# A two-layer hybrid decoder on one core: weight splits, squares, rotary angles and early weight loads put in other places

## The chip, the core and the metric

The kernel runs as one program on one core of a Trainium2 chip. The core has a matrix engine (TensorE, PE in the profile; PEld is its weight load), VectorE (DVE), ScalarE (ACT), GpSimd (POOL) and SyncE (SP), each with its own instruction stream. Every DMA of this kernel is issued from SP. The metric is the device time of one execution in microseconds; of several runs the median counts.

## What is computed

512 tokens of 1024 channels pass through two layers in float32. In each layer:

```python
h = rmsnorm(x, norm_mix_pre)
proj = h @ w_in                      # q, k, v | r, k, v, lora_w, lora_a, lora_g | two gates
q = rope(q, positions); k = rope(k, positions)
y_att = sliding_window_attention(q, k, v, att_sinks) @ w_o_att
y_rw = rwkv7_time_mix(rw, ...) @ w_o_rw
x = x + rmsnorm((sigmoid(gate_a) * y_att + sigmoid(gate_b) * y_rw) @ w_out, norm_mix_post)
h = rmsnorm(x, norm_ffn_pre)
ua, ub = split(causal_dwconv(h @ w_up, conv_w, conv_b))      # 2 x 2816 channels
x = x + rmsnorm((gelu(ua) * ub) @ w_down, norm_ffn_post)
e = p_i @ w_ple                                              # 256 -> 1024: the embeddings
x = x + rmsnorm(sigmoid(x @ w_ple_gate) * e, norm_ple)
```

## The kernel before, in words

**Tiling.** All activations lie channel-first: a tile is 128 channels by 512 tokens, x has eight (KT = 8). A half is 256 tokens (HALVES). Every float32 operand is split into a high and a low part, and a product is three matmuls (`mm3`, lines 245 to 247): high weight by high activation, high by low, low by high. So a projection tile of 1024 channels in is 24 matmuls, of 512 columns or, by halves, of 256.

**A weight's way.** SP issues the DMA of a raw weight into SBUF; ScalarE copies it into the high part (`wh`, or `kwh` where the weight is kept for both halves; line 125 is the helper that issues every ACTIVATE); VectorE subtracts to get the low part (`wl` at line 155, `kwl` at line 128). Raw and split weights go round in buffers by class: "m" has two raw buffers and three of each part, "f" one and two, "x" takes both classes by turns (`whole` and `load_w` take a class, `keep_w` keeps a split weight in a pool given to it, with raws through the slots of "m" and "f"). A DMA whose raw buffer is still being read waits on SP, and everything behind it on SP waits too.

**PSUM.** Tiles are named `pm` (two buffers), `pf` (one), `lead`, `half` and `scores` (three together), `ple` and others (two). A tile gets its buffer when the last reader of the tile before it is done.

**Stages of a layer.** `lead` runs the opening tiles of a projection by halves, so that the first half can begin when half of the tokens are normed: in the mixer the low-rank and key tiles, ahead of the up projection five conv tiles. `seam` ties a norm to such an opening. Behind the mixer's opening stand the low-rank gates (`lora`), then, in layer 0 only, the angles of the rotary embedding (`trig`: sine and cosine of positions, stored through `csd` and read back as `sinT` and `cosT`), then the attention; copies `qs<-q` rotate the halves of q and k. Behind the up projection's opening come eight embedding tiles (`w_ple`, classes "m" and "f" by turns), each copied by ScalarE to `e` and stored to `ed`; then `ffn` with the conv tiles m and 22 + m (FT = 22) by turns. Five conv tiles are done by the opening; the next two, 24 and 3, have their weights loaded at the start of `ffn` (`ahead`). Each conv tile is multiplied on VectorE by the norm's scale (`un<-pf` or `un<-pm`), and three steps make the convolution (`cv`).

**The turn into the gate.** The down projection (`dn`) is a `lin` with seven whole tiles and the last by halves. Between them four of the eight gate weights are kept in advance. `fin` is its result; `post_norm` norms a half of it (`rstd`, then `yo` and `x` on VectorE) and `scaled` splits it into `xh` and `xl`. Then the gate `pg`, a `lin` with deep = 3: tiles 0 to 2 together, then the other five, first for the first half, then for the second, where tiles 3 to 7 use `half` buffers. `ple` is its end: it loads the embedding back (`yo<-ed`), takes the tanh (`tg`) and multiplies. In `turn` the second half's norm stands behind `last_lo`, the last low part made.

**What sets the order.** The text is only a priority: a list scheduler (the Tile framework) sorts instructions of all engines by it. `turn` raises the priority of what is in it, and `tc.issue_after(i)` holds what is in it back until i is issued.

## Time and profile before

| | us |
|---|---|
| median of three runs | 2374.32 (2373.6 to 2386.13) |
| the profiled execution | 2373.8 |
| its span, first to last instruction | 2371.9 |
| TensorE busy | 2228.8 (94%) |
| VectorE busy | 1554.1 (66%) |
| ScalarE busy | 1123.6 (47%) |

TensorE's mean granted clock is 0.971 of full speed. The two levels seen in the rows are 2.4 GHz (1.0) and 1.2 GHz. Busy times overlap between engines; a wait of TensorE counts where nothing else of it can run meanwhile. Rows of the listing in time give start, duration, engine, line, operation, output and inputs, and in brackets the idle time of the engine ahead and what ended it; equal neighbours are one row with xN.

### The profile page before, as it was taken

What the parts mean: (1) busy time and instruction counts of PE and PEld (TensorE: products, weight loads), DVE (VectorE), ACT (ScalarE), POOL (GpSimd) and SP (SyncE); (2) the same over time, 40 slices, a digit from 0 to 9 for tenths busy, and PEclk for the clock granted to TensorE, in tenths of its full rate; (3) what the DMA queues carried; (4) which work ended last, traced back from release to release, by engine and by line L of the source; (5) the groups of instructions that cost most, each with busy time, mean ns of one, the idle gap of its engine ahead of it and who ended that gap; (6) DMA issues with size and microseconds to landing.
All of it is one profiled execution on the core that took longest, in us unless ns stands there. A gap on an engine that the chain in (4) does not pass through costs nothing.

```text
span 2371.9 us, 39518 instructions
## 1 busy us (share of the span) xinstructions
PE 2228.8 (94%) x14340; PEld 1756.5 (74%) x14340; DVE 1554.1 (66%) x3683; ACT 1123.6 (47%) x2450; POOL 27.3 (1%) x86
## 2 busy tenths in 40 slices
PE   7699999999999999999898999998999999999986
PEld 6566776667779788888795667766677888888876
DVE  4765588677566777733777646788666667776355
ACT  4466456445444554532355554555543445444332
POOL 1000000000000000000000000000000000000000
PEclk9899999789999999999899999999999999999998
DMA  3532332335571333333235233333356623333431
GB/s 123 153 91 99 107 94 73 85 97 181 164 249 60 118 101 96 95 116 100 80 124 153 83 104 101 88 94 92 110 158 210 215 70 103 98 98 102 125 98 36
DMA packets 206818, 269.39 MB, mean 114 GB/s; under 512 B 72096, under 2 KB 88992, under 8 KB 206624
## 3 DMA queue, kind: packets, MB, share of 16 engines
q1 hardware_dynamic: 206624, 266.88, 36.5%
q8 instruction: 113, 1.85, 0.3%
q14 instruction: 81, 0.66, 0.1%
HBM read 218.95 MB, written 42.47 MB: 110 GB/s over the span
## 4 chain that ended last, share of the span: by engine, by line
PE 71%; DVE 12%; DMA 8%; ACT 6%; issue 3%; SPq 1%; POOL 0%; DVEq 0%; ACTq 0%; POOLq 0%
PE pm L245 12%; PE pm L247 12%; PE pm L246 12%; PE pf L245 6%; PE pf L247 6%; PE pf L246 6%; DVE wl L155 2%; DMA w<-in_w_dn_dram 1%; PE A L117 1%; ACT wh L125 1%; PE pT L550 1%; PE scores L117 1%; SPq L122 1%; PE xs L773 1%; PE sp L780 1%
## 5 line engine op out<-in xcount | busy, mean ns | idle before, releaser
L125 ACT ACTIVATE wh<-w 128x512 fp32r<-128x512 f32 (+1 forms) x590 | 353.6, 606 | 567.9 <-PE pm L246 172.5
L155 DVE TENSOR_TENSOR wl<-w,wh 128x512 fp32r<-128x512 f32 (+2 forms) x574 | 376.7, 661 | 266.8 <-ACT wh L125 261.7
L247 PE MATMUL pm<-hh,wl 128*128 128x512 f32 x1040 | 422.7, 406 | 5.7 <-DVE wl L155 5.6
L245 PE MATMUL pm<-hh,wh 128*128 128x512 f32 x1040 | 424.3, 408 | 2.2 <-DVE Z L694 0.9
L246 PE MATMUL pm<-hl,wh 128*128 128x512 f32 x1040 | 420.0, 404 | 0.2 <-DVE hl L128 0.2
L245 PE MATMUL pf<-hh,wh 128*128 128x512 f32 x544 | 221.5, 407 | 21.0 <-ACT wh L125 16.7
L247 PEld LDWEIGHTS pm<-hh,wl 128*128 128x128 f32 x1040 | 197.3, 190 | 52.4 <-DVE wl L155 9.0
L245 PEld LDWEIGHTS pm<-hh,wh 128*128 128x128 f32 x1040 | 197.4, 190 | 49.0 <-issue 5.4
L246 PEld LDWEIGHTS pm<-hl,wh 128*128 128x128 f32 x1040 | 197.6, 190 | 46.4 <-issue 6.6
L247 PE MATMUL pf<-hh,wl 128*128 128x512 f32 x544 | 219.4, 403 | 0.9 <-DVE wl L155 0.6
L246 PE MATMUL pf<-hl,wh 128*128 128x512 f32 x544 | 218.2, 401 | 0.0
L134 DVE SCALAR_TENSOR_TENSOR cv<-un,vec,cv 128x511 f32<-128x511 f32 (+1 forms) x176 | 130.9, 749 | 23.4 <-ACT cv L125 20.8
L245 PEld LDWEIGHTS pf<-hh,wh 128*128 128x128 f32 x544 | 104.1, 191 | 51.4 <-ACT wh L125 25.3
L247 PEld LDWEIGHTS pf<-hh,wl 128*128 128x128 f32 x544 | 103.8, 191 | 31.2 <-DVE wl L155 6.4
L246 PEld LDWEIGHTS pf<-hl,wh 128*128 128x128 f32 x544 | 104.0, 191 | 21.8 <-issue 1.8
L245 PE MATMUL pm<-uh,wh 128*128 128x512 f32 (+1 forms) x248 | 89.2, 360 | 2.8 <-ACT wh L125 2.8
L247 PE MATMUL pm<-uh,wl 128*128 128x512 f32 (+1 forms) x248 | 89.1, 359 | 0.0
L246 PE MATMUL pm<-ul,wh 128*128 128x512 f32 (+1 forms) x248 | 88.9, 359 | 0.0
L125 ACT ACTIVATE cv<-un,vec 128x512 f32<-128x512 f32 x88 | 71.5, 814 | 31.9 <-DVE un L128 31.9
L128 DVE TENSOR_TENSOR acc<-acc,sq 128x256 f32<-128x256 f32 (+1 forms) x114 | 50.2, 465 | 40.3 <-ACT sq L125 39.6
L528 DVE CUSTOM_DVE_ANT_0 sm<-scores,tmask 128x256 f32<-128x256 f32 (+1 forms) x128 | 43.5, 385 | 36.6 <-PE scores L117 36.5
L692 DVE TENSOR_TENSOR Z<-rin,Z 128x126 f32<-128x126 f32 (+22 forms) x248 | 62.3, 251 | 4.3
(402 smaller groups left out, 4418.0 us busy)
## 6 DMA issues: line engine op xcount, KB each, us to landing
w<-in_w_up_dram SPq DMA_DIRECT2D x156, 256.0 KB
w<-in_w_dn_dram SPq DMA_DIRECT2D x80, 256.0 KB
w<-in_w_q_dram SPq DMA_DIRECT2D x32, 256.0 KB
w<-in_w_ga_dram SPq DMA_DIRECT2D x32, 256.0 KB
w<-in_w_k_dram SPq DMA_DIRECT2D x32, 256.0 KB
w<-in_w_r_dram SPq DMA_DIRECT2D x32, 256.0 KB
w<-in_w_v_dram SPq DMA_DIRECT2D x32, 256.0 KB
w<-in_w_gb_dram SPq DMA_DIRECT2D x32, 256.0 KB
```

Of the source, the lines that this page charges most:

```text
L117: i = self.nc.tensor.matmul(out, l, r, start=start, stop=stop)
L122: return self.nc.sync.dma_start(out=out, in_=in_)
L125: return self.nc.scalar.activation(out=out, in_=in_, func=func, **kw)
L128: return self.nc.vector.tensor_tensor(out=out, in0=in0, in1=in1, op=op)
L134: return self.nc.vector.scalar_tensor_tensor(out=out, in0=in0, scalar=s, in1=in1, op0=op0, op1=op1)
L155: self.nc.vector.tensor_tensor(out=wl, in0=w, in1=wh.bitcast(F32), op=ALU.subtract)
L245: mm(ps, wh, ah, start=start, stop=False)
L246: mm(ps, wh, al, start=False, stop=False)
L247: mm(ps, wl, ah, start=False, stop=stop)
L528: nc.vector.tensor_tensor_reduce(out=sm[i][:, par * 256:par * 256 + KW], in0=scs[par][:, x * 256:x * 256 + KW], in1=tm, scale=1.0, scalar= ...
L550: nc.tensor.transpose(tp[:, i * P:(i + 1) * P], sm[i][:, par * 256 + b * P:par * 256 + (b + 1) * P], self.ident)
L692: nc.vector.tensor_tensor(out=tv, in0=rin[:, jj:jj + 1, jj + 1:].broadcast_to([P, n, nt]), in1=zt[:, :n, jj:jj + 1].broadcast_to([P, n, nt ...
```

## The change

Five things move; nothing is added to what is computed.

1. `lead` and `lin` note a fixed matmul (`self.pin`: the last of the third row of products in an opening, of the sixth in a `lin`). The second half's norm in `turn` now stands behind it, and behind the last high and low part (`behind`).
2. The split weights of the second layer's opening stand behind the last high and low part.
3. The angles are made in the first pool, behind the mixer's opening and ahead of the low-rank gates.
4. Gate weights 4 to 7 are loaded after the first half of the down projection's last tile, behind the last high and low part of the first norm.
5. The weights of conv tiles 24 and 3 are loaded ahead of the last two embeddings, with their classes exchanged, and these two embeddings take class "m".

```diff
@@ lead
         for hs in HALVES:
             for k in range(n):
                 for key, ps, width, w in out:
-                    self.mm3(ps[:width, hs], w[k], tuple(x[:, hs] for x in act[k]), k == 0, k == n - 1)
+                    i = self.mm3(ps[:width, hs], w[k], tuple(x[:, hs] for x in act[k]), k == 0, k == n - 1)
+                if k == 2:
+                    self.pin = i
@@ scaled
-            self.act(hi, x[:, hs])
+            self.last_hi = self.act(hi, x[:, hs]).ins
...
-            self.act(hi, x[:, hs], scale=g)
+            self.last_hi = self.act(hi, x[:, hs], scale=g).ins
@@ run, opening of a layer
-            next(ld)
+            with self.behind() if l else ExitStack():
+                next(ld)
             if l == 0:
                 next(ld)
             self.seam(tail, xs, "pre", hb, ld, A, S)
+            if l == 0:
+                self.trig(self.alloc(xpool, "T", 8), self.csd)
...
                 sg = self.lora(l, N, WA)
-                if l == 0:
-                    self.trig(N, self.csd)
                 self.attention(l, ap, N, F, sg)
@@ lin
-                ws = ws or [self.load_wk(src(n), S)]
+                ws = [self.load_wk(src(n), S)] if ws is None else ws
...
+                        if k == 5:
+                            self.pin = x_
@@ embeddings
-                self.cls = "mf"[m % 2]
+                if m == 6:
+                    ahead = {FT + 2: self.whole(a["w_up"][l, FT + 2], P, "m"), 3: self.whole(a["w_up"][l, 3], P, "f")}
+                self.cls = "mf"[m % 2] if m < 6 else "m"
@@ gate
-            gw += [self.whole(a["w_pg"][l, m], P, "mf"[m - 4]) for m in range(4, 6)]
-            gw += [self.keep_w(a["w_pg"][l, m], P, G) for m in range(6, KT)]
...
                 if hs is HALVES[0]:
                     next(dn)
+                    if hs is HALVES[0]:
+                        with self.behind():
+                            gw += [self.whole(a["w_pg"][l, m], P, "mf"[m - 4]) for m in range(4, 6)]
+                            gw += [self.keep_w(a["w_pg"][l, m], P, G) for m in range(6, KT)]
@@ turn and behind
             if hs is HALVES[1]:
-                st.enter_context(self.tc.issue_after(self.last_lo))
+                st.enter_context(self.behind())
+                st.enter_context(self.tc.issue_after(self.pin))
             yield
+
+    @contextmanager
+    def behind(self):
+
+        with self.tc.issue_after(self.last_lo), self.tc.issue_after(self.last_hi):
+            yield
@@ ffn
-                ps = self.PM("mf"[m > FT])
+                ps = self.PM("fm"[m > FT])
...
-        ahead = {FT + 2: self.whole(a["w_up"][l, FT + 2], P, "f"), 3: self.whole(a["w_up"][l, 3], P, "m")}
```

How this moves instructions, at three places.

On SP, at the start of layer 0's attention, before (`csd` is the store of the angles, `sinT` and `cosT` read them back, `qs` are copies of q and k, `w` a raw weight):

```order
L122 DMA w<-in_w_q_dram 128x512
L122 DMA w<-in_w_g_dram 128x256
L122 DMA qs<-q 32x512 x3
L122 DMA csd<-rr 128x512
L122 DMA qs<-q 32x512 x2
L122 DMA csd<-rr 128x512
L122 DMA sinT<-csd 128x512
L122 DMA qs<-q 32x512 x2
L122 DMA cosT<-csd 128x512
L122 DMA qs<-q 32x512 x13
L122 DMA w<-in_w_q_dram 128x512
```

and now:

```order
L122 DMA csd<-rr 128x512
L122 DMA w<-in_w_g_dram 128x256
L122 DMA csd<-rr 128x512
L122 DMA sinT<-csd 128x512
L122 DMA cosT<-csd 128x512
L122 DMA w<-in_w_q_dram 128x512
L122 DMA w<-in_w_g_dram 128x256
L122 DMA w<-in_w_q_dram 128x512
L122 DMA qs<-q 32x512 x16
L122 DMA w<-in_w_q_dram 128x512
```

The store of the angles and its two loads are now ahead of these weights of q and of all the `qs` copies.

On VectorE, at the third conv tile of layer 0, before (`un_8496` belongs to conv tile 24, `un_8533` to conv tile 3; `wl_8543` is the first low weight of the third conv tile, tile 25):

```order
L134 SCALAR_TENSOR_TENSOR cv_8464<-un_8465,vec_87,cv_8464 128x510
L134 SCALAR_TENSOR_TENSOR cv_8495<-un_8496,vec_87,cv_8495 128x511
L128 TENSOR_TENSOR ul_8461<-cv_8446,uh_8460 128x512
L134 SCALAR_TENSOR_TENSOR cv_8495<-un_8496,vec_87,cv_8495 128x510
L155 TENSOR_TENSOR wl_8543<-w_8539,wh_8541 128x512
```

and now:

```order
L134 SCALAR_TENSOR_TENSOR cv_8464<-un_8465,vec_87,cv_8464 128x510
L128 TENSOR_TENSOR un_8496<-pm_8470,rs_85 128x512
L128 TENSOR_TENSOR ul_8461<-cv_8446,uh_8460 128x512
L128 TENSOR_TENSOR un_8533<-pf_8507,rs_85 128x512
L134 SCALAR_TENSOR_TENSOR cv_8495<-un_8496,vec_87,cv_8495 128x511
L155 TENSOR_TENSOR wl_8543<-w_8539,wh_8541 128x512
```

Conv tile 3 now runs first, and the low weight stands behind the `un` of both tiles and one `cv`.

On ScalarE, at the end of layer 0's down projection, before (`yo_10250` is its last tile by halves, `xh` the high part of the normed x, `kwh` and `wh` gate weights, but `wh_11932` the next layer's opening):

```order
L125 ACTIVATE wh_11178<-w_11176 128x512
L125 ACTIVATE wh_11190<-w_11188 128x512
L125 ACTIVATE yo_10250<-pm_11279 128x256
L125 ACTIVATE sq_11347<-pm_11279 128x256
L125 ACTIVATE kwh_11202<-w_11200 128x512
L125 ACTIVATE kwh_11208<-w_11206 128x512
L125 ACTIVATE wh_11932<-w_11930 128x512
L125 ACTIVATE kwh_11214<-w_11212 128x512
L125 ACTIVATE xh_11154<-x_7538 128x256
L125 ACTIVATE xh_11156<-x_7540 128x256
```

and now:

```order
L125 ACTIVATE xh_11154<-x_7538 128x256
L125 ACTIVATE xh_11156<-x_7540 128x256
L125 ACTIVATE xh_11158<-x_7542 128x256
L125 ACTIVATE yo_10250<-pm_11231 128x256
L125 ACTIVATE xh_11160<-x_7544 128x256
L125 ACTIVATE sq_11299<-pm_11231 128x256
L125 ACTIVATE xh_11162<-x_7546 128x256
L125 ACTIVATE xh_11164<-x_7548 128x256
L125 ACTIVATE xh_11166<-x_7550 128x256
L125 ACTIVATE xh_11168<-x_7552 128x256
L125 ACTIVATE wh_11304<-w_11302 128x512
L125 ACTIVATE wh_11310<-w_11308 128x512
```

The eight copies of x are between and behind the last down tile's, and the late gate weights (`wh_11304` and on) stand behind them. Further on, on ScalarE, the rows up to the tanh of gate tile 2, whose PSUM buffer gate tile 5 takes next, before:

```order
L125 ACTIVATE tg_11430<-pm_11351 128x256
L125 ACTIVATE xh_11160<-x_7544 128x256
L125 ACTIVATE xh_11162<-x_7546 128x256
L125 ACTIVATE xh_11164<-x_7548 128x256
L125 ACTIVATE xh_11166<-x_7550 128x256
L125 ACTIVATE xh_11168<-x_7552 128x256
L125 ACTIVATE acc_11226<-yo_11218 128x256
L125 ACTIVATE sq_11434<-yo_11219 128x256
L125 ACTIVATE tg_11437<-pm_11352 128x256
```

and now:

```order
L125 ACTIVATE xh_11168<-x_7552 128x256
L125 ACTIVATE wh_11932<-w_11930 128x512
L125 ACTIVATE kwh_11334<-w_11332 128x512
L125 ACTIVATE kwh_11340<-w_11338 128x512
L125 ACTIVATE wh_11938<-w_11936 128x512
L125 ACTIVATE kwh_11346<-w_11344 128x512
L125 ACTIVATE acc_11178<-yo_11170 128x256
L125 ACTIVATE sq_11434<-yo_11171 128x256
L125 ACTIVATE tg_11437<-pm_11352 128x256
```

The copies of gate weights 6 and 7 and of the next layer's opening weights are now ahead of the two that read the returned embeddings (`acc<-yo`, `sq<-yo`), and of this tanh.

## Rows read from the trace of the kernel before

**Rows 1.** Page, part 1: busy us, share of the span, instructions.

```profile
PE 2228.8 (94%) x14340; PEld 1756.5 (74%) x14340; DVE 1554.1 (66%) x3683; ACT 1123.6 (47%) x2450; POOL 27.3 (1%) x86
```

**Rows 2.** Waits of TensorE: engine, line, releaser; us, times, longest us.

```profile
PE pf L245 <- ACT wh L125: 16.7, 11, 3.5
PE pf L245 <- ACT xh L125: 13.1, 2, 7.3
...
PE ssq L279 <- DVE acc L128: 9.2, 2, 5.1
```

**Rows 3.** Table by stretches: length, PE, PEld, DVE, ACT, POOL, PEclk, DMA, GB/s.

```profile
47.70:117.60 69.90, 50.58 (x257) 40.43 (x256) 52.88 (x104) 29.08 (x52) 2.84 (x7) 0.89 0.43 130
1226.40:1287.30 60.90, 50.19 (x259) 39.79 (x258) 44.98 (x88) 26.98 (x49) 2.84 (x7) 0.97 0.47 142
```

**Rows 4.** Listing in time, ScalarE: start, us, instruction, [idle before, releaser].

```profile
8.72 0.51 ACT L125 ACTIVATE hh<-x,vec 128x256 fp32r<-128x256 f32 x1 [0.94 <-DMA x<-in_xT_dram]
...
74.15 1.28 ACT L125 ACT_TABLE_LOAD   x1
75.44 0.63 ACT L125 ACTIVATE rr<-rr 128x512 f32<-128x512 f32 x1
```

**Rows 5.** Listing in time, SP's queue, attention of layer 0.

```profile
79.93 0.33 SPq L122 DMA_DIRECT2D csd<-rr  x1
...
82.60 8.57 SPq L122 DMA_DIRECT2D qs<-q  x13
91.22 0.57 SPq L122 DMA_DIRECT2D w<-in_w_q_dram  x1
```

**Rows 6.** Listing in time, TensorE, scores of layer 0.

```profile
90.60 0.80 PE L117 MATMUL scores<-q 64*128 64x128 f32 x4 [8.71 <-DVE q L128]
```

**Rows 7.** Listing in time, TensorE, first conv tiles of layer 0.

```profile
793.28 0.80 PE L245 MATMUL pf<-hh,wh 128*128 128x512 f32 x1 [3.50 <-ACT wh L125]
...
798.90 0.40 PE L245 MATMUL pm<-hh,wh 128*128 128x512 f32 x1
...
804.97 0.50 PE L247 MATMUL pm<-hh,wl 128*128 128x512 f32 x1
```

**Rows 8.** Listing in time, VectorE, first conv tiles of layer 0.

```profile
803.57 0.74 DVE L134 SCALAR_TENSOR_TENSOR cv<-un,vec,cv 128x510 f32<-128x510 f32 x1
804.23 0.69 DVE L155 TENSOR_TENSOR wl<-w,wh 128x512 fp32r<-128x512 f32 x1
```

**Rows 9.** Listing in time, TensorE, down projection into gate, layer 0.

```profile
1137.41 0.98 PE L279 MATMUL ssq<-ones,acc 128*128 128x1 f32 x4 [5.12 <-DVE acc L128]
1144.25 0.58 PE L245 MATMUL pf<-xh,kwh 128*128 128x256 f32 x1 [5.85 <-ACT xh L125]
...
1150.50 0.28 PE L245 MATMUL pf<-xh,kwh 128*128 128x256 f32 x1
1150.62 0.28 PE L246 MATMUL pf<-xl,kwh 128*128 128x256 f32 x1
```

**Rows 10.** Listing in time, ScalarE, gate of layer 0, then of layer 1.

```profile
1143.26 0.63 ACT L125 ACTIVATE kwh<-w 128x512 fp32r<-128x512 f32 x1 [2.35 <-DMA w<-in_w_pg_dram]
...
1161.48 0.36 ACT L125 ACTIVATE tg<-pm 128x256 f32<-128x256 f32 x1
...
1195.82 0.39 ACT L125 ACTIVATE tg<-half 128x256 f32<-128x256 f32 x1 [1.13 <-PE half L247]
...
2326.38 0.39 ACT L125 ACTIVATE tg<-pm 128x256 f32<-128x256 f32 x1 [1.59 <-PE pm L247]
...
2349.49 0.38 ACT L125 ACTIVATE tg<-half 128x256 f32<-128x256 f32 x1 [1.59 <-PE half L247]
```

**Rows 11.** Listing in time, SP's queue, gate of layer 0.

```profile
1145.02 8.25 SPq L122 DMA_DIRECT2D yo<-ed  x16
```

**Rows 12.** Listing in time, TensorE, gate and end of layer 1.

```profile
2300.72 0.58 PE L245 MATMUL pf<-xh,kwh 128*128 128x256 f32 x1 [7.29 <-ACT xh L125]
...
2352.46 1.19 PE L285 MATMUL rstd<-ident,nry 128*128 128x128 f32 x4 [2.73 <-DVE nry L134]
```

More of the change, by code (lines that the diff above doesn't have):

```diff
@@ L246, in mm3 @@
         mm(ps, wh, al, start=False, stop=False)
-        mm(ps, wl, ah, start=False, stop=stop)
+        return mm(ps, wl, ah, start=False, stop=stop).ins
     def proj(self, src, act, width=P, cls=None, key=None):
@@ L960, in lin @@
                         for i in range(deep):
-                            self.mm3(pss[i][:, hs], ws[i][k], tuple(x[:, hs] for x in act[k]), k == 0, k == len(act) - 1)
+                            x_ = self.mm3(pss[i][:, hs], ws[i][k], tuple(x[:, hs] for x in act[k]), k == 0, k == len(act) - 1)
+                        if k == 5:
+                            self.pin = x_
                     for i in range(len(ws)):
@@ L1007, in run @@
             self.cls = "x"
-            u = self.ffn(l, hb, G, Y, S)
+            u = self.ffn(l, hb, G, Y, S, ahead)
             ys = [Y("yo") for _ in range(KT)]
@@ L1068, in seam, with ffn @@
             self.token_scale(accs[0])
-    def ffn(self, l, h, G, Y, F):
+    def ffn(self, l, h, G, Y, F, ahead):
         a, vv = self.a, self.vv
```

## The prediction

> **What bounds the kernel now.** I read the page's totals first: TensorE is busy 2228.8 of 2371.9 us [rows 1]. The 143 us in which it idles, and the stretches in which it runs at the lower of its two clock levels, are all that a change of order can win. The list of waits on TensorE comes next [rows 2]: the first conv tile waits for weight copies (longest 3.5), the gate's first tile for the copies of x (13.1 in two waits), a sum of squares for acc (9.2 in two waits). Then the table by stretches, for the same work in both layers: from the sums of squares behind the opening tiles to the first low-rank gate tile takes 69.90 us in layer 0 at a granted clock of 0.89 and 60.90 us in layer 1 at 0.97 [rows 3]. Last come the listings in order of time around each wait, engine by engine.
>
> One execution gives the durations: 2373.8 us, 1.9 of them outside the span. The median shown is 0.5 higher, less than my terms are good for, so I add nothing.
>
> **The change, part by part.**
>
> *Opening of layer 0.* ScalarE stands 0.94 us for x before its copy at 8.72 [rows 4]; the weight splits behind the input copies fill that gap, and the opening tiles run back to back behind it, so everything starts about 0.9 us sooner, **-0.9**. If the split weights were late instead, TensorE's first wait would grow by as much: 0 to -0.9.
>
> *Angles in the first pool (layer 0).* Before, SP reaches the store of the angles (csd) at 79.93, stands behind its wait, then has two tables and 15 qs copies, thirteen of them in one row of 8.57 us, ahead of the next w_q, which it issues only at 91.22 [rows 5]. TensorE waits 8.71 before the scores at 90.60 [rows 6]. After, csd, sinT and cosT are off the queue before the attention's weights, and the order is that of layer 1, where no angles are made. So the same work of layer 1 is my price: 69.90 - 60.90 = 9.0 us [rows 3], **-9.0**, low clock included. The bound on the other side: the sine's table load (1.28 us [rows 4], at 74.15) now stands ahead of work that the low-rank tiles wait for, and has to be undone for the next function: one load on the path is **+1.3**; with none of it hidden and a second load, +2.6.
>
> The row at 74.15 lasts 1.28 and the next ACTIVATE starts at 75.44, right behind it [rows 4]. The Trainium skill (ScalarE: Activation LUTs, section What ACT_TABLE_LOAD costs) gives a switch about 1.28 us of load and 1.38 us of drain; by the row there is no drain to be seen, and by the page the term above would be +2.7 in place of +1.3, the sum 1.4 later.
>
> *Up weights among the embeddings (each layer).* Before, the second weight chunk of the first conv tile is copied late: a wait of 3.50 at 793.28, and twelve matmuls that take 5.62 us to 798.90; at full clock 26 take 6.07 (798.90 to 804.97), so twelve cost 2.8 and the clock costs 2.8 more [rows 7]. After, both weights are there, but the last two embedding weights stand on SP behind three stores of finished embeddings. By the durations of this stretch that gives five waits of 0.2 to 1.1 us on TensorE before the first conv tile, which starts 2.0 us later. Two tiles then run without a break to about 799.8. The third tile's weight subtract (wl) now stands on VectorE behind the second tile's un, one cv and two more: 3.6 us at 0.6 to 0.7 from start to start [rows 8]. So its third matmul comes at 803.4, before at 804.97: -1.5. That wait is 3.1 us long, and after 3.50 the clock fell [rows 7]; a fall costs up to 2.8, of which I take 1.8. Layer 0 **+0.3**. In layer 1 the wait removed is shorter than 3.5 [rows 2], so **+1.3**. Bounds -1.5 to +3 each.
>
> *Norm into gate, layer 0.* Before, VectorE does the whole first norm, then weight subtracts, then acc: TensorE waits 5.12 and again 5.85 for xh, which stands on ScalarE behind copies of late gate weights (the copy at 1143.26 itself waited 2.35 for its DMA [rows 10]); 27 matmuls then take 6.25 us where 0.12 each would be 3.2 [rows 9]. After, the copies of x go between the steps of the norm and the four late gate weights behind them. Gate tiles 0 to 2 start where the down tile ends, at 1132.3 (1137.41 less 5.12 [rows 9]): both waits and the low clock, 14 us, are gone from that place. What is late next: tiles 3 and 4, then the second halves of tiles 3, 4 and 5 run ahead, to about 1156.4. Tile 5 takes the PSUM buffer of tile 2, which is free once ScalarE's tg has read it, and that tg stands behind two copies that need the embeddings back (yo<-ed, 16 loads that take SP 8.25 us [rows 11]). SP reaches these loads only behind the gate and lead weights, whose buffers come free late: about 1157 now, 1145.02 before. Landed at 1160, tg at 1161.4, before at 1161.48 [rows 10]. So a new wait of **5 us** stands before tile 5, which starts when it did before. The three half tiles that have moved ahead (3 x 24 x 0.12 = 8.6 us) are then missing behind it: the second halves of tiles 6 and 7 are put behind an opening tile of layer 1, whose weight subtract stands behind the norm on VectorE, and behind a buffer of the three half tiles; TensorE idles 7 to 8 us there. The last half tile's tg was at 1195.82 [rows 10]; the walk gives 1195.1 with no fall of the clock and 1199.6 with one after each wait; the nine opening matmuls done early give back 1.1. Net -1.6 to +2.9; both waits are as long as those after which it fell [rows 7, 9], so I take the upper part, **+2**. If the half tiles could not run ahead, the first wait would be 8.6 longer and the second shorter by them: the end would be the same.
>
> *The same in layer 1, and the tail.* The wait for xh is 7.29 [rows 12], and the new wait before tile 5 is again about 4.9, so tile 7's first half ends about as before, by the walk 0.3 later (its tg was at 2326.38 [rows 10]). Behind it there is no next layer: before, 23.1 us to the last tg at 2349.49; after, 72 + 48 matmuls at 0.12 are 14.4, a wait of 2.4 for a tg, and 0.4 for what lies between: 17.2. That is -5.9; with the 0.3 and 1.8 for a fall of the clock after the 4.9, **-3.8**. The first half's sum of squares stood behind the last tile, and TensorE waits 2.73 for its rstd [rows 12]; now it is 48 matmuls ahead of the end, the norm starts right behind the last tile: **-2.7**. Bounds for both -8.5 to -2.
>
> *Second half's squares behind a fixed matmul (seam into the up projection).* 21 matmuls later, 2.5 us, on engines that idle there: 0; if not covered, up to +2.5 once.
>
> Sum: -0.9 - 9.0 + 1.3 + 0.3 + 1.3 + 2 - 3.8 - 2.7 = -11.5, so 2373.8 - 11.5 = **2362**.
>
> **The rivals.**
> 1. *The turns give all they promise.* Nothing takes the place of the waits: 14 us in layer 0, in layer 1 4.1 + 7.3 + 3.0 = 14.4 [rows 2, 9, 12]. For it: the copies of x really come first. Against it: two PSUM buffers, and SP late with yo<-ed. 2373.8 - 0.9 - 7.7 + 1.6 - 14 - 14.4 - 2.7 = 2336.
> 2. *Waits only move.* The half tiles ahead end no sooner in either layer, the tail's gain goes into a later last tile, only the attention's 7.7 and the start's 0.9 stay, with 1.6 + 2 for embeddings and layer 0: 2369. For it: the late yo loads hold both ends of the gate.
> 3. *The angles were not it.* qs copies and weights keep SP as long as before, with the angles a few us earlier: the 9.0 is gone, the table load is not. 2362 + 9 = 2371. Against it: layer 1, same queue order, without the waits.
> 4. *Slower: the clock.* At the lower level a matmul of 256 columns takes about 0.21, at the higher 0.12 [rows 9]. If TensorE stays at the lower level behind the new 5 us wait, through the tiles that run up to the next wait (3 x 24 + 72 = 144 matmuls, 13 us in each layer) instead of the 27 matmuls that rows 9 show, 2 x 13 less the 2 to 4 already in the sum give 2362 + 23 to 26 = 2387. It decides from some 130 low matmuls per layer. Against it: in rows 7 and 9 the clock was back within 6.3 us of dense work. The Trainium skill (TensorE: Matmul & The Clock Gate, section A second HAM failure mode: psum-queue depth-cycling) says that small idles between groups of matmuls, from cycling through PSUM, make the clock swing and cost throughput; it speaks for this rival, since the change swaps two long waits for several that hang on PSUM buffers. No row read here shows it: those that I have show falls behind waits of 3.5 us and more [rows 7, 9].
>
> **How the numbers follow.** A measurement here tells 0.5%, 11.9 us, from no change: faster lies below 2362.4, slower above 2386.2. Forecast 0.50 (its own range 2354 to 2370, from all bounds of the clock's falls, so a little over half of it faster), rival 1 or a good part of it 0.20 (2336 to 2353), rival 2 0.16, rival 3 0.07, rival 4 0.07. Faster 0.27 + 0.20 = 0.47; same 0.23 + 0.16 + 0.07 = 0.46; slower 0.07. The range leaves out the deeper half of rival 1 and rival 4: 2347 to 2375.
>
> **What would show it.** Right: in layer 0 no wait of 8.7 before the scores and the first stretch of rows 3 at about 62 us; no waits of 5.12 and 5.85 between the down tile and the gate, but one of some 5 us before gate tile 5, released by a tg, and one of 6 to 7 before the second half of tile 6; in the conv's third tile a wait for wl of some 3 us; at the end an rstd without the 2.73. Wrong: yo<-ed issued before 1150 (then rival 1), an attention stretch still near 70 us (rival 3), long stretches at the lower level behind the new waits (rival 4).

## The result and the profile after

The changed kernel takes 2357.6 us (median of six runs, 2351.7 to 2363.6) against 2374.0 for the kernel before in runs beside it. The ratio is 0.9922, with a 95% interval from 0.9896 to 0.9949: faster, by more than the 0.5% that can be told. The forecast was 2362, the range 2347 to 2375. The profiled execution took 2361.0, with this span and these busy times (page, first lines):

```profile
span 2359.2 us, 39516 instructions
...
PE 2230.6 (95%) x14340; PEld 1757.7 (75%) x14340; DVE 1555.0 (66%) x3683; ACT 1123.3 (48%) x2450; POOL 26.5 (1%) x86
```

TensorE works as long as before [rows 1], 2230.6 us; what has shrunk is the time between. The list of its waits (us in total, times, longest) answers to [rows 2]:

```profile
...
PE pf L247 <- ACT wh L125: 10.9, 10, 3.2
PE pm L247 <- ACT tg L125: 10.2, 2, 5.5
PE pm L249 <- DVE wl L155: 9.2, 7, 3.7
...
PE pm L249 <- DVE kwl L128: 5.8, 1, 5.8
```

The two groups of [rows 2] at the turn into the gate, for xh (13.1) and for acc (9.2), are gone. In their place stand a wait for tg (10.2 in two), one for kwl (5.8) and more for wl (9.2 in seven). The wait for wh ahead of pf is down from 16.7 to 10.9.

To see where the time went, I cut both executions into stages by the number of the TensorE instruction: each program has 14,340, and a stage that the change leaves alone is then the same work. A second execution of the changed kernel was profiled later (below). The stage "gate of layer 0 with layer 1's opening", for instance, runs from instruction 6600, in the down projection, to 7640, in layer 1's attention.

| stage | forecast | first execution | second |
|---|---|---|---|
| start to the sums of squares of layer 0 | -0.9 | -0.3 | -0.5 |
| to the first low-rank gate tile [rows 3] | -7.7 | -9.7 | -7.9 |
| embeddings to third conv tile, layer 0 | +0.3 | +0.5 | +0.4 |
| the same, layer 1 | +1.3 | -1.3 | -1.6 |
| gate of layer 0 with layer 1's opening | +2.0 | +0.8 | -1.4 |
| gate of layer 1 to the end | -6.5 | -7.0 | -5.3 |
| all the rest, order unchanged | 0 | +4.4 | -6.8 |
| whole | -11.5 | -12.6 | -23.0 |

**The opening.** What fills the gap on ScalarE is not the weight splits: squares of x (`sq<-x`) now stand between the input copies, and the first weight split behind them (`kwh`) comes at 14.60. The first two rows are of the changed kernel, the third of the kernel before:

```profile
7.28 0.40 ACT L125 ACTIVATE sq<-x 128x256 f32<-128x256 f32 x1
...
14.60 0.61 ACT L125 ACTIVATE kwh<-raw 128x512 fp32r<-128x512 f32 x1
```

```profile
16.06 0.61 ACT L125 ACTIVATE kwh<-raw 128x512 fp32r<-128x512 f32 x1
```

**Attention of layer 0.** The table by stretches gives, for the interval of [rows 3], 60.16 us at full clock where 69.90 stood:

```profile
47.44:107.60 60.16, 49.03 (x257) 38.43 (x256) 44.47 (x86) 28.40 (x50) 2.83 (x7) 1.00 0.45 135
```

SP's queue, which answers to [rows 5], now has sinT and cosT long before the copies; all qs copies are one run, and the w_q behind them is issued at 75.63, not 91.22:

```profile
48.26 0.33 SPq L122 DMA_DIRECT2D sinT<-csd  x1
48.63 0.43 SPq L122 DMA_DIRECT2D cosT<-csd  x1
...
64.48 11.05 SPq L122 DMA_DIRECT2D qs<-q  x16
75.63 0.53 SPq L122 DMA_DIRECT2D w<-in_w_q_dram  x1
```

So the scores wait 0.77 us, not the 8.71 of [rows 6]:

```profile
81.40 0.49 PE L117 MATMUL scores<-q 64*128 64x128 f32 x4 [0.77 <-DVE q L128]
```

**The conv.** The wait of 3.50 before the first conv tile [rows 7] is 0.69; at the third tile's third matmul a wait for wl is new, in layer 0 (790.30) and in layer 1 (1965.93). On VectorE the subtract that makes this wl stands behind the `un` of the tile before it:

```profile
775.01 0.50 PE L247 MATMUL pf<-hh,wh 128*128 128x512 f32 x1 [0.69 <-ACT e L125]
...
790.30 0.80 PE L249 MATMUL pm<-hh,wl 128*128 128x512 f32 x1 [3.66 <-DVE wl L155]
...
1965.93 0.51 PE L249 MATMUL pf<-hh,wl 128*128 128x512 f32 x1 [1.99 <-DVE wl L155]
```

```profile
788.30 0.68 DVE L128 TENSOR_TENSOR un<-pf,rs 128x512 f32<-128x512 f32 x1
...
789.56 0.68 DVE L155 TENSOR_TENSOR wl<-w,wh 128x512 fp32r<-128x512 f32 x1
```

**The gate.** TensorE's listing shows the new waits: before tile 5 in layer 0, with 25 matmuls some 0.21 apart behind it (the lower clock level, against 0.12 at the higher); for kwl at the third matmul of layer 1's opening, which stands ahead of tile 6's second half, with 23 such matmuls behind it; and in layer 1 before tile 5 (17 such matmuls) and before tile 6's second half. At the end the rstd of [rows 12] has no wait any more:

```profile
1149.79 0.58 PE L247 MATMUL pm<-xh,wh 128*128 128x256 f32 x1 [5.46 <-ACT tg L125]
1150.16 0.41 PE L248 MATMUL pm<-xl,wh 128*128 128x256 f32 x1
1150.38 0.41 PE L249 MATMUL pm<-xh,wl 128*128 128x256 f32 x1
...
1177.40 0.58 PE L249 MATMUL pm<-hh,kwl 128*128 128x256 f32 x1 [5.81 <-DVE kwl L128]
...
2312.18 0.43 PE L247 MATMUL pm<-xh,wh 128*128 128x256 f32 x1 [4.70 <-ACT tg L125]
...
2333.88 0.39 PE L247 MATMUL half<-xh,kwh 128*128 128x256 f32 x1 [2.25 <-ACT tg L125]
...
2339.73 0.60 PE L287 MATMUL rstd<-ident,nry 128*128 128x128 f32 x4
```

The embeddings that the tanh's neighbours on ScalarE need are loaded from 1144.96; before it was 1145.02 [rows 11], but the down tile now ends at 1119.7 and ended at 1132.3 then. Against that end the loads are 12.5 us later:

```profile
1144.96 7.54 SPq L122 DMA_DIRECT2D yo<-ed  x16
```

And on ScalarE the row that TensorE waits for, tg at 1149.37, stands behind the copy of yo that waited for them, with VectorE's step between:

```profile
1148.51 0.42 ACT L125 ACTIVATE acc<-yo 128x256 f32<-128x256 f32 x1 [2.03 <-DVE yo L134]
...
1149.37 0.36 ACT L125 ACTIVATE tg<-pm 128x256 f32<-128x256 f32 x1
```

### The profile page after: what moved, and what is told of

The parts are those of the page before. It is cut to its first block, busy times and chain, and to the rows that moved or that the text cites. A ratio compares the mean times of both kernels' runs of the same rounds, so it can differ in the third digit from the quotient of the medians.

```text
span 2359.2 us, 39516 instructions
## 1 busy us (share of the span) xinstructions
PE 2230.6 (95%) x14340; PEld 1757.7 (75%) x14340; DVE 1555.0 (66%) x3683; ACT 1123.3 (48%) x2450; POOL 26.5 (1%) x86
## 5 line engine op out<-in xcount | busy, mean ns | idle before, releaser
L134 DVE SCALAR_TENSOR_TENSOR cv<-un,vec,cv 128x510 f32<-128x510 f32 (+1 forms) x176 | 131.0, 750 | 24.6 <-ACT cv L125 22.0
L128 DVE TENSOR_TENSOR un<-pm,rs 128x512 f32<-128x512 f32 x56 | 38.5, 690 | 41.2 <-PE pm L249 41.1
```

The source lines that it names most:

```text
L128: return self.nc.vector.tensor_tensor(out=out, in0=in0, in1=in1, op=op)
L134: return self.nc.vector.scalar_tensor_tensor(out=out, in0=in0, scalar=s, in1=in1, op0=op0, op1=op1)
```

## The experiments

Twelve more programs ran, eleven variants and the changed kernel once more, in three sets, each with runs of the kernel before on the same chip (medians 2372.6, 2371.9 and 2371.3). The chip differs from set to set, so times of different sets are best compared by their ratios to the kernel before. None of the variants leaves out a part of the computation.

### One part undone at a time

**Angles back behind the low-rank gates**, else as changed:

```diff
-            if l == 0:
-                self.trig(self.alloc(xpool, "T", 8), self.csd)
...
                 sg = self.lora(l, N, WA)
+                if l == 0:
+                    self.trig(N, self.csd)
```

> The changed kernel with the angles made behind the low-rank gates again, as before; all else as changed. Theory (SP held by the store of the angles, with the qs copies behind it, costs layer 0 the difference to layer 1): the wait before the scores of layer 0 comes back with 8 to 9 us, and from the sums of squares to the first low-rank gate tile it takes 69 to 71 us, against 60.3 in the changed kernel; time 2366 to 2369 against 2357.6. Rival (most of the stretch's gain was the clock, which fell by chance in the execution profiled before): the stretch stays under 64 us and the time within 3 us of 2357.6.

Measured: 2365.3 us (12 runs), ratio to before 0.9975 (0.9953 to 0.9997). The stretch is back at 69.31 us and the scores wait 8.65; these are the table by stretches and TensorE's listing of this kernel:

```profile
46.18:115.49 69.31, 50.49 (x258) 40.41 (x256) 52.79 (x104) 29.13 (x52) 2.84 (x7) 0.89 0.43 130
```

```profile
88.99 0.80 PE L117 MATMUL scores<-q 64*128 64x128 f32 x4 [8.65 <-DVE q L128]
```

The theory holds in the stage, and in the time (0.7 below its 2366). The clock (0.89) is part of the price, but follows the wait: it is back with it.

**Gate weights 4 to 7 loaded ahead of the norm again**:

```diff
             xa = [(G("xh", F32R), G("xl", F32R)) for _ in range(KT)]
+            gw += [self.whole(a["w_pg"][l, m], P, "mf"[m - 4]) for m in range(4, 6)]
+            gw += [self.keep_w(a["w_pg"][l, m], P, G) for m in range(6, KT)]
...
-                        with self.behind():
-                            gw += [self.whole(a["w_pg"][l, m], P, "mf"[m - 4]) for m in range(4, 6)]
-                            gw += [self.keep_w(a["w_pg"][l, m], P, G) for m in range(6, KT)]
```

> The changed kernel with gate weights 4 to 7 loaded ahead of the norm again, as before; all else as changed. Theory (the removed waits of the turn came back as a wait for a PSUM buffer and one for a low weight, in layer 0 in full): the waits for acc and xh between down tile and gate come back with 4 to 7 us each, the waits of 5.5 for tg and 5.8 for kwl go; layer 0 loses nothing or gains up to 2, layer 1 loses 4 to 7; time 2360 to 2365. Rival (the early copies of x are the change's main gain and the waits behind them cost little): time above 2370.

Measured: 2366.5 us (12 runs), ratio 0.9971 (0.9950 to 0.9992). TensorE's listing has one wait per layer, of 12 us, where I expected two of 4 to 7:

```profile
1131.30 0.58 PE L247 MATMUL pf<-xh,kwh 128*128 128x256 f32 x1 [11.94 <-ACT xh L125]
...
2298.14 0.58 PE L247 MATMUL pf<-xh,kwh 128*128 128x256 f32 x1 [11.86 <-ACT xh L125]
```

On ScalarE the copies of x stand behind the last late gate weight, which waited for its DMA:

```profile
1130.31 0.63 ACT L125 ACTIVATE kwh<-w 128x512 fp32r<-128x512 f32 x1 [2.86 <-DMA w<-in_w_pg_dram]
1130.85 1.32 ACT L125 ACTIVATE xh<-x 128x256 fp32r<-128x256 f32 x4
```

The waits for tg and kwl are gone. The gate's first matmul comes 11.6 us later than in the changed kernel, but from instruction 6600 to the end of layer 1's opening (7409) it takes 118.7 us, in the changed kernel 119.9 and 118.8: layer 0 gains 0.1 to 1.2 from the undoing. In layer 1, from instruction 13800 to the end, 91.4 us stand against 83.2 and 85.0, so it loses 6.4 to 8.1. Of 23.8 us of waits that the part removes, these 6 to 8 are its gain: the theory, with layer 1 up to 1.1 us and the time 1.5 us over its bounds; the rival's 2370 and more did not come.

**Early conv weights back behind the embeddings, classes as before**:

```diff
-                if m == 6:
-                    ahead = {FT + 2: self.whole(a["w_up"][l, FT + 2], P, "m"), 3: self.whole(a["w_up"][l, 3], P, "f")}
-                self.cls = "mf"[m % 2] if m < 6 else "m"
+                self.cls = "mf"[m % 2]
...
+            ahead = {FT + 2: self.whole(a["w_up"][l, FT + 2], P, "f"), 3: self.whole(a["w_up"][l, 3], P, "m")}
...
-                ps = self.PM("fm"[m > FT])
+                ps = self.PM("mf"[m > FT])
```

> The changed kernel with the two early conv weights loaded behind the embeddings again, classes as before; all else as changed. Theory (a wait of 3.2 to 3.5 with a fall of the clock was swapped for one of 2 to 3.7 behind the norm's scale on VectorE): the wait for wh before the first conv tile is back with 3 to 3.5, the wait for wl before the third tile goes; from the last embedding to the third conv tile within 1 us in layer 0, up to 3 us longer in layer 1; time 2357 to 2361. Rival (the early loads are worth their whole removed wait in both layers): 2364 or more.

Measured: 2358.1 us (10 runs), ratio 0.9946 (0.9923 to 0.9969). The waits for wh are back, in layer 0 with 3.38 and in layer 1 with 3.37:

```profile
783.37 0.50 PE L247 MATMUL pf<-hh,wh 128*128 128x512 f32 x1 [3.38 <-ACT wh L125]
```

The wait for wl at the third tile is gone. The stage takes 27.6 us in layer 0 (28.9 and 28.7 in the changed kernel's two executions) and 35.1 in layer 1 (33.0 and 32.7). One wait was swapped for another: the part costs 1.2 us in layer 0 (a little over the 1 expected) and gains 2.2 in layer 1, where the new wait is 2.0 long.

**The two small parts**, first together (the second half's norm behind the last low part alone, and the second layer's opening weights free):

```diff
-                st.enter_context(self.behind())
-                st.enter_context(self.tc.issue_after(self.pin))
+                st.enter_context(self.tc.issue_after(self.last_lo))
...
-            with self.behind() if l else ExitStack():
-                next(ld)
+            next(ld)
```

> The changed kernel without the fixed matmul ahead of the second half's norm and without the opening's split weights behind the last low and high part. Theory (both stand on engines that idle there): 2356 to 2360, every wait over 3 us where it was. Rival (the fixed matmul keeps VectorE free for what the gate waits for): the gate's waits grow by 2 us or more per layer, time 2362 or more.

Measured: 2364.4 us (10 runs), ratio 0.9960 (0.9944 to 0.9976), where I expected at most 2360, while the profiled execution (2359.0) has the changed kernel's stages to about a microsecond. The time is the rival's (2362 or more), the longer waits at the gate that it rests on did not come. So in the last set I ran them apart, with the changed kernel beside them:

> The changed kernel once more, for a second profiled execution and as the measure for the other three of this set. Theory (what differs between executions is the granted clock in stages that the change does not touch, above all the scans of the mixer): time 2354 to 2361; the stages at the embeddings, the gate and the attention of layer 0 within 1 us of the first execution, the scans up to 6 us off. Rival (the first set's chip or hour was kind to it): 2362 or more.

> The changed kernel without the fixed matmul and the last high part ahead of the second half's norm (behind the last low part alone, as before). Theory (the 6.8 us by which the run without both small parts was slower is the opening: its squares go back between the input copies, and a clock that happened to be lower): the opening's first matmul about 1 us later, all else alike, time within 3 us of the second run of the changed kernel. Rival (the fixed matmul is worth it at the norms): 4 to 8 us slower than that run, with longer waits between norm and gate.

> The changed kernel with the second layer's opening weights no longer behind the last low and high part. Theory (they are needed late, and stand on engines that idle): no wait changes by over 1 us, time within 3 us of the second run of the changed kernel. Rival (they push the gate's copies back on ScalarE): the wait before gate tile 5 of layer 0 grows by 1 us or more, 3 us or more slower.

Measured: the changed kernel again 2353.4 (9 runs, ratio 0.9927, 0.9902 to 0.9951), half a microsecond under the theory's range. Its second execution keeps the waits at gate and conv to 0.5 us; the stretch to the first low-rank gate tile is 1.9 longer, and layer 1's scans take 102.8 us in place of 111.1, more than the 6 that I had allowed. Both miss the theory's bounds. The other two: without the fixed matmul 2359.1 (12 runs, 0.9958, 0.9936 to 0.9979), with the opening's weights free 2360.2 (12 runs, 0.9951, 0.9931 to 0.9971). Without the fixed matmul the first matmul comes at 16.7 (15.5 with it), as expected. Otherwise the stages that a part touches are within half a microsecond of the longer of the changed kernel's two executions; only layer 1's embeddings without the fixed matmul are 1.6 longer, by a fall of the clock. The waits before gate tile 5 are no longer (up to 4.8 and 5.5, against 5.4). The medians lie 6 and 7 us above that of the changed kernel, so both theories (within 3 us) missed, and the rivals have the time right but not the longer waits that they give as the cause. The intervals overlap the changed kernel's, though all three runs without a part lie on the same side (0.9951 to 0.9960 against 0.9922 and 0.9927). The profiles don't show what would cost these 6 us; whether the two parts are worth them stays open.

**The angles alone** in the kernel before:

```diff
             self.seam(tail, xs, "pre", hb, ld, A, S)
+            if l == 0:
+                self.trig(self.alloc(xpool, "T", 8), self.csd)
...
-                if l == 0:
-                    self.trig(N, self.csd)
```

> The kernel before, with the angles alone moved to the first pool. Theory (this part stands for itself): from the sums of squares to the first low-rank gate tile 60 to 62 us in place of 69.9, all later stages as before, time 8 to 10 us under the kernel before, ratio 0.996. Rival (it gains only with the other parts, or the later wait for weights takes it back): less than 4 us.

Measured: 2363.6 us (12 runs) against 2371.3, ratio 0.9960 (0.9940 to 0.9981), 7.7 us. The stretch of [rows 3] takes 63.12, 6.8 less than before:

```profile
47.75:110.87 63.12, 50.36 (x256) 39.77 (x256) 44.56 (x86) 28.52 (x50) 2.83 (x7) 0.96 0.43 132
```

The theory holds, with the stretch 1.1 us over its 60 to 62 and the time 0.3 under its gain of 8 to 10; this part alone is about half of the whole gain. Over all twelve profiled executions with the angles moved, the stretch takes 60.1 to 63.1 us, 62.3 in the mean.

### What holds the gate now

**Embeddings 0 to 2 of the first half loaded ahead of the late gate weights**:

```diff
                 tg = S("tg")
-                self.dma(y, row(ed, m)[:, hs])
+                if not (m < 3 and hs is HALVES[0]):
+                    self.dma(y, row(ed, m)[:, hs])
...
                     if hs is HALVES[0]:
+                        for m in range(3):
+                            self.dma(ys[m][:, hs], row(ed, m)[:, hs])
                         with self.behind():
```

> The changed kernel, and the first halves of embeddings 0 to 2 are loaded back ahead of the late gate weights. Theory (the new wait before gate tile 5 is for a tanh that stands on ScalarE behind copies that need embeddings, and SP reaches their loads only behind weights): the wait of 5.5 in layer 0 and of 4.7 in layer 1 falls under 1.5; tile 6's second half no longer stands behind an opening tile, so the wait of 5.8 for kwl goes too; each turn gains 4 to 7 us, time 2344 to 2351. Rival (two PSUM buffers and VectorE's second norm hold the gate; the loads only happen to be late): a wait of about the same length for tg, one tile later; time within 3 us of 2357.6.

Measured: 2351.1 us (6 runs), ratio 0.9900 (0.9868 to 0.9932). SP now issues three loads 18.5 us sooner, among the gate weights:

```profile
1126.41 1.38 SPq L122 DMA_DIRECT2D yo<-ed  x3
```

The wait before tile 5 is 1.30 in layer 0, and gone in layer 1, but in layer 0 one of 7.82 has come up before tile 6's second half, again for a tg:

```profile
1149.82 0.39 PE L247 MATMUL pm<-xh,kwh 128*128 128x256 f32 x1 [1.30 <-ACT tg L125]
...
1172.00 0.58 PE L247 MATMUL half<-xh,kwh 128*128 128x256 f32 x1 [7.82 <-ACT tg L125]
```

So the first step of the theory is right (late loads, not the two PSUM buffers as such), and the second was wrong in layer 0: the wait for kwl went and another took its place. The stage of layer 0's gate gains 4.5 and 2.3 us against the changed kernel's two executions, layer 1's end 6.3 and 8.0; the interval of the time overlaps the changed kernel's, so the stages carry this reading. On ScalarE the tanh of tile 3's second half at 1171.58 (the tg<-half below) stands behind squares and copies that wait for VectorE, which does the first half's norm until then. That VectorE's norm is what holds them is read from the order of the rows; the next kernel tests it:

```profile
1169.34 0.40 ACT L125 ACTIVATE acc<-yo 128x256 f32<-128x256 f32 x1
...
1171.26 0.42 ACT L125 ACTIVATE sq<-yo 128x256 f32<-128x256 f32 x1 [0.94 <-DVE yo L134]
1171.58 0.37 ACT L125 ACTIVATE tg<-half 128x256 f32<-128x256 f32 x1
```

**Second halves of tiles 3 to 5 evaluated ahead of those of tiles 0 to 2**, on top of the early loads:

```diff
+                    early = (3, 4, 5) if deep == 3 and not one else ()
+                    for i in early:
+                        ps = self.PS("half")
+                        self.proj_half(ps, ws[i], act, hs)
+                        done(n + i, ps, hs, i == 3)
                     pss = [self.PM("x") if i < 3 else self.PS("half") for i in range(deep)]
```

The loop behind leaves these three tiles out, and the sum of squares of that half begins with tile 3.

> As the run with the early embeddings (2351.1), and in the gate's second half tiles 3 to 5, whose matmuls run early anyway, are also evaluated ahead of tiles 0 to 2. Theory (there the wait of 7.8 in layer 0 before tile 6's second half was for a tanh of tile 3 that stood on ScalarE behind squares which need VectorE, busy with the first half's norm): those tanhs now run before the norm, the wait falls under 1.5 in both layers, layer 0 gains 3 to 6 and layer 1 about 2; time 2343 to 2347. Rival (the norm of the first half on VectorE sets the start of layer 1's opening whatever stands before it): the wait moves behind the gate, to the first opening matmuls, with 5 us or more; time within 3 us of 2351.

Measured: 2345.0 us (6 runs), ratio 0.9864 (0.9840 to 0.9889). The three tanhs run before the norm (ScalarE, two from 1150.87 and the third at 1153.05):

```profile
1150.87 0.64 ACT L125 ACTIVATE tg<-half 128x256 f32<-128x256 f32 x2
```

and the wait of 7.82 is gone. Layer 1's opening waits 1.20 for its first matmul, so the rival is out; in layer 1 the 2.25 is gone, but the first rstd waits 2.73 again, as in [rows 12]:

```profile
1169.40 0.39 PE L247 MATMUL lead<-hh,wh 128*128 128x256 f32 x1 [1.20 <-ACT tg L125]
...
2309.47 0.35 PE L287 MATMUL rstd<-ident,nry 128*128 128x128 f32 x1 [2.73 <-DVE nry L134]
```

The table's stage from the gate of layer 0 through layer 1's opening takes 156.4 us, 165.0 with the early loads alone, 169.5 in the changed kernel: 8.6 us against 3 to 6 expected. Layer 1 gained nothing, where about 2 were expected. Here the interval of the time (0.9840 to 0.9889) lies clear of the changed kernel's.

**The third conv tile's weights first**, on the changed kernel:

```diff
-                ps = self.proj(a["w_up"][l, m], h, key=m)
+                with self.tc.high_priority(offset=PRIO) if m == FT + 3 else ExitStack():
+                    ps = self.proj(a["w_up"][l, m], h, key=m)
```

> The changed kernel, and the weights of the third conv tile (tile 25) are given high priority, so that their subtract stands on VectorE ahead of the scale of the two tiles before. Theory (the wait of 3.7 and 2.0 for wl at the third tile's third matmul is VectorE's order, and a fall of the clock comes with it in layer 0): the wait goes; from the first conv tile's start to the third matmul of the third tile 12 us in place of 12.4 to 16, time 2352 to 2356 against 2357.6. Rival (the weight itself is late, since SP loads it behind the stores of the embeddings): VectorE now stands for it ahead of the opening's conv steps, a later tile waits instead, time within 2 us of 2357.6 or up to 5 longer.

Measured: 2353.1 us (6 runs), ratio 0.9914 (0.9889 to 0.9939). The wait for wl is gone; two small ones for un stand in its place:

```profile
783.40 0.50 PE L247 MATMUL pm<-hh,wh 128*128 128x512 f32 x1 [0.67 <-DVE un L128]
...
795.61 0.47 PE L247 MATMUL pm<-hh,wh 128*128 128x512 f32 x1 [1.01 <-DVE un L128]
```

In layer 0 the stage falls from 28.9 to 24.4 us, with the fall of the clock that the wait had brought. But it ends ahead of the second of the two small waits: counted to instruction 5400, behind both, 55.3 us become 52.2, so 3.1 us remain. In layer 1 the stage stays (33.0 before, 32.8 now), since two waits for un of 0.9 have replaced the one of 2.0. The theory holds for layer 0; of the time I can't say more than that it lies where it was expected.

**All three**:

> The changed kernel with the early embeddings, the early evaluation of tiles 3 to 5 and the third conv tile's weights first. Theory (the three waits lie in different stages, so their gains add): time 2338 to 2344, none of the waits of 5.5, 5.8, 4.7, 3.7 left. Rival (each gain is eaten by the next stage's own bound): 2346 or more.

Measured: 2333.9 us (4 runs, 2330.2 to 2337.6), ratio to before 0.9830 (0.9808 to 0.9851). This version beats both kernels. Its longest waits on TensorE:

```profile
PE lead L247 <- ACT kwh L125: 15.4, 1, 15.4
PE pm L247 <- ACT wh L125: 12.0, 6, 4.4
PE pf L247 <- ACT wh L125: 11.4, 10, 3.5
PE rstd L287 <- DVE nry L134: 11.0, 5, 7.8
```

The first is the start of the kernel. The 5.81 for kwl and the 3.66 for wl are gone, and of the waits for tg two of 1.2 are left in layer 0. By stages the gains add: layer 0's gate with layer 1's opening takes 156.1 us (156.4 without the conv part), layer 1's end 76.9 as without it, and the first conv tiles of layer 0 gain 2.6. The time is 4 us under what I had expected, and 11 under the kernel without the conv part, more than that part's stage explains; the two intervals overlap.

## Why the prediction was right, step by step

**The attention** was the largest term, and pricing it by layer 1 of the same kernel was right: the stretch is 9.7 and 7.9 us shorter in two executions, 6.8 with the angles alone, and 7.5 in the mean of all twelve with the angles moved, where the terms gave 7.7 net. The wait of 8.71 is gone, as walked; one for weights that layer 1 has too, 3.3 us there, has grown in layer 0 from 0.5 to 3.2, and belongs to layer 1's price. The table load that I put on the path (+1.3) can't be seen there: the sine's own load now runs at 30.43, in the opening; the one for the next function runs at 55.31, ScalarE's next instruction starts 1.30 later, and TensorE has no wait over 0.53 between the sums of squares and the scores but the one of 0.77:

```profile
55.31 1.28 ACT L125 ACT_TABLE_LOAD   x1
56.61 0.63 ACT L125 ACTIVATE wa<-wa 64x512 f32<-64x512 f32 x1
```

Here too there is no drain behind the load, where the Trainium skill (ScalarE: Activation LUTs, section What ACT_TABLE_LOAD costs) counts about 1.38 us. No run shows the +1.3 by itself; what keeps the mean of layer 0 above layer 1's 60.9 stays open.

**The gate of layer 0** went as walked. Both waits of [rows 9] were removed and came back elsewhere: a wait before tile 5 of 5.46 (walked: 5), for a tg behind yo<-ed, with the loads 25.2 us after the down tile's end (walked: 25), and one of 5.81 for kwl behind the norm (walked: 6 to 7). The clock fell after both. The sum was +2, measured +0.8 and -1.4; counted only to the end of layer 1's opening it is +1.5 and +0.4, and the rest of the second execution's figure lies in layer 1's attention, behind the opening. The second cause is confirmed only in part: with the early loads the 5.81 went, but a 7.82 for another tg came, and with the tanhs evaluated ahead of the norm that went too. So what stood there was VectorE's norm, through whichever instruction came behind it in an engine's order.

**Layer 1's gate and tail** were -6.5 and are -7.0 and -5.3: waits of 4.70 (4.9 expected) and 2.25 (2.4), with a fall of the clock after the first, and no 2.73 at the end. The last tg is 3.9 and 2.2 us earlier (3.8 expected), what follows it 3.1 shorter in both (2.7).

**The opening** had its size about right and its filler wrong. The first matmul is 1.5 and 1.2 us earlier, but the sums of squares only 0.3 and 0.5: the opening's first 200 instructions take 27.25 and 26.83 us, before 26.05. The difference is the clock at the start: 28 and 24 matmuls run at the lower level before it rises, 14 in the kernel before. In five variants with the same early first matmul (13 to 16 matmuls at the lower level) the sums of squares come 1.4 to 1.6 us sooner, and over all ten executions with this opening the gain is 0.3 to 1.6, 1.0 in the mean. The gap on ScalarE was filled by the squares of x and not by weight splits, and the run without the fixed matmul, where the first matmul is back at 16.7, shows which part did it: the one that the prediction put at 0.

**The embeddings of layer 1** were +1.3 and are -1.3 and -1.6. The step that failed is that I carried layer 0's new wait of 3.1 over to layer 1 with a fall of the clock. There it is 1.99 and 1.98, and the matmuls behind it ran at the higher level in both executions; that this was not certain is shown in the last section. In layer 0 it is 3.66 (3.1 walked), and the clock did fall.

**The rivals.** Nothing of rival 1's 28 us could be had, since two new waits came with it; but the experiments with the loads and the order of the halves recover most of it (the stage of layer 0's gate falls from 168.7 us before to 156.4, layer 1's end from 90.2 to 76.9), so two PSUM buffers did not force the waits. Rival 2 was near for layer 0 alone. Rival 3 is excluded by the run with the angles undone. Rival 4 did not come: behind the 5.46 and the 5.81 the clock was low for 25 and 23 matmuls, as for the 27 before, and not for 130. The rule of the Trainium skill that was named for it (TensorE: Matmul & The Clock Gate, section A second HAM failure mode: psum-queue depth-cycling) is borne out only so far as these falls; over the whole span the granted clock is 0.976, before 0.971. Two sums of the prediction are slightly off, without effect on the forecast: the net of layer 0's gate comes out of its terms as -1.8 to +2.7 (given as -1.6 to +2.9), rival 4's cost as 22 to 24 (23 to 26).

That the first execution (-12.6) came so near to the sum (-11.5) is luck: the stages that the change touches gained 17.0 and 16.3 us in two executions, and the rest gave 4.4 back in one and 6.8 more in the other. The medians moved by 16.4 and 17.9 us, as the touched stages did, so the sum was some 5 us short; the largest piece of that are layer 1's embeddings, 2.6 and 2.9 us.

## What to carry to other kernels

Where the same program runs a stage twice and one copy of it is slower, the other is the best price for the difference; look in the queue that issues the DMAs for what only the slow copy has. A wait that is removed on an engine with its results queued in order can come back at the next shared thing, as two did here: before moving loads behind a norm, ask which later loads stand behind them in the same queue, and whose buffers wait for those. Try evaluating results in the order in which they are computed: here three finished tiles held their PSUM buffers behind results that were not ready, and the reordering took 8.6 us out of the stage.

## What the runs showed of the hardware

Stretches that no part touches vary by half and more of what the change is worth (16.4 us). In the mixer of layer 0, TensorE's instructions 2300 to 2500 (matmuls of the scan and of a projection, in the same order in all kernels) take from 12.79 to 21.35 us. These are the table by stretches of the kernel before and of the kernel with the angles alone:

```profile
421.71:442.96 21.25, 21.25 (x201) 15.09 (x200) 5.22 (x13) 3.82 (x13) 0.00 (x0) 0.50 0.24 59
```

```profile
416.56:429.35 12.79, 12.79 (x202) 9.30 (x201) 5.51 (x14) 3.34 (x11) 0.00 (x0) 0.99 0.37 95
```

TensorE is busy throughout, without a wait, and the granted clock is 0.50 or 0.99: the whole stretch at the lower level or at the higher. Three other executions lie between (15.0 to 17.3 us). Before it stands a wait of 2.38 us for AR, in the kernel before and in the one with the gate weights undone alike; the first then ran at 0.50, the second at 1.00. In layer 1 the scans (instructions 9440 to 10400) take 101.7 to 115.7 us in the same way. So one execution's total says little about a change of 10 us; the stages do.

A short wait is no surer. In nine executions the same wait of 1.98 or 1.99 us for wl stands in layer 1's conv. In three of them (the angles undone, the fixed matmul undone, the early embeddings) the clock fell within the next dozen matmuls, which cost some 1.6 us; in the other six it did not. This is the one with the early embeddings, whose matmuls behind the wait are 0.43 apart (0.23 at the higher level):

```profile
1966.42 0.50 PE L249 MATMUL pf<-hh,wl 128*128 128x512 f32 x1 [1.98 <-DVE wl L155]
...
1967.84 0.63 PE L247 MATMUL pf<-hh,wh 128*128 128x512 f32 x1
1968.27 0.63 PE L248 MATMUL pf<-hl,wh 128*128 128x512 f32 x1
```
